# Branch gates of a hybrid decoder layer as seven half-size products for two tiles, in a stage ahead of the mixers

## Chip, cores and metric

The kernel runs on one core of one Trainium2 chip. The time is the device time of one execution in microseconds, as a median of repeated runs. TensorE (PE) multiplies and writes to PSUM; VectorE (DVE), ScalarE (ACT) and GpSimd (POOL) do the elementwise work; SyncE's queue (SP) issues most transfers.

## What is computed

One decoder layer in float32 on 1056 tokens (1024 of a prompt, 32 of a sample group), width 1024. The part that matters, from the reference:

```
h = x + 0.5 * swiglu(rmsnorm(x, g_ffn1), w_ffn1_in, w_ffn1_out)
u = rmsnorm(h, g_mix)
z = split(u @ w_in)                  # attention q, k, v; GLA inputs; memory queries z_mq
o_swa, o_gla, o_mem = mixers(z)      # each (tokens, 512)
mq = z_mq.reshape(B, T, MEM_HEADS, HEAD_DIM)
gates = sigmoid(u @ w_gate).reshape(B, T, N_BRANCH, D_MODEL)     # 3 x 1024 features
br = einsum('btnc,ncd->btnd', stack([o_swa, o_gla, o_mem], axis=2), w_branch)
h = h + sum(gates * br, axis=2) @ w_out
h = h + 0.5 * swiglu(rmsnorm(h, g_ffn2), w_ffn2_in, w_ffn2_out)
y = rmsnorm(h, g_final)
```

## The kernel before

**Layout.** Features lie on the 128 partitions, tokens on the free axis. A slab is one 128 x 1056 buffer; there are 34 (`NSLAB`), given out as they come free. Every float32 product is three matmuls in a reduced format: weights and data are each split into a rounded high part and the rest (`split`, L206 to L209, `weights`, L177 to L192: ACT casts, DVE or POOL subtracts), and `product` (L194 to L204) adds high x high, high x low and low x high. A plain 128-feature tile with depth 1024 is 8 x 3 matmuls for each chunk of tokens: 72 of 352 columns, when the tokens are cut in thirds. Weights come through three pairs of buffers, `raw`, `whi` and `wlo` (`WBUFS`).

**Seven half-size products.** In both feed-forward layers two output tiles a and b are made together from seven products of half depth (`weight_forms`, L395; `pair_products`, L419; the tokens' sums from `Forms.sums`, L365). For each of two pairs of token quarters that is 7 x 12 matmuls of 264 columns, so 168 for two tiles. Their 20 pairs follow on two tiles of each layer that are done the plain way (`plain_products`, L459).

**Stages.** `ffn` (L697) ends with `out_product` (L652), whose last block of depth goes by token thirds, so that `norm_after` (L294) can norm one third while the next is multiplied. Norm steps wait in `k.later` and are taken one at a time with `k.step()`, between products. `Mix.run` (L1620) then makes the projections of u and, between their products, takes a step of five streams with `k.tick()`: GLA, window attention, its sample scores, memory attention, the combination. PE's order is as the program is written; the other engines' orders are made by a planner ahead of time, by readiness and program order. Four memory query projections (`mem_proj`, L1093) are spread over the GLA part. The streams still open when `run` ends are taken on in `gated_branches` (L1650).

**`gated_branches`.** It takes the branches in the order GLA, memory, attention (i = 0, 1, 2), and eight output tiles t in each. For each tile and each third c, `gate` (L1680) makes 24 matmuls on u and a sigmoid on ACT, and `values` (L1690) 12 matmuls on the branch's output; DVE multiplies the two and POOL adds into `merged`. `gate` ticks the streams once, in the first pass (i = 0) twice. At t = 0, and for the last two tiles, three gate products run ahead of the values. At t = 6 of the first pass the streams are flushed and the next branch's output is loaded. The splits `mp` of the merged tiles (L1807) and `w_out` follow.

## Time and profile before

| | |
|---|---|
| median of 3 runs | 3049.06 us |
| lowest and highest | 3039.51 and 3050.46 us |
| profiled execution | 3053.2 us |
| its span, first to last instruction | 3051.4 us |
| matmuls of PE | 21035 |
| PE busy | 2932.9 us |
| granted TensorE clock, mean | 0.975 of 2.4 GHz |

A profiled execution gives each instruction's start and duration. A matmul's duration includes its way through the array, and neighbours overlap; what a matmul costs in a dense stretch is the length of the stretch divided by their count. The clock is granted at 2.4 or 1.2 GHz; a mean between says how the stretch was divided.

### The profile page before, as it was taken

What the parts mean: (1) busy time and instruction counts of PE and PEld (TensorE: products, weight loads), DVE (VectorE), ACT (ScalarE), POOL (GpSimd) and SP (SyncE); (2) the same over time, 40 slices, a digit from 0 to 9 for tenths busy, and PEclk for the clock granted to TensorE, in tenths of its full rate; (3) what the DMA queues carried; (4) which work ended last, traced back from release to release, by engine and by line L of the source; (5) the groups of instructions that cost most, each with busy time, mean ns of one, the idle gap of its engine ahead of it and who ended that gap; (6) DMA issues with size and microseconds to landing.
All of it is one profiled execution on the core that took longest, in us unless ns stands there. A gap on an engine that the chain in (4) does not pass through costs nothing. (4 is left out here: it accounts for less than half of the span.)

```text
span 3051.4 us, 51965 instructions
## 1 busy us (share of the span) xinstructions
PE 2932.9 (96%) x21035; PEld 2867.0 (94%) x21035; DVE 1415.2 (46%) x2581; ACT 1013.6 (33%) x2007; POOL 972.3 (32%) x835
## 2 busy tenths in 40 slices
PE   8999999999999999899998889999999999999999
PEld 7999999899999999888897789999999999999998
DVE  7544444454424445656556551213246544444544
ACT  5433333221345433232332321212234433333212
POOL 4533331110401114637447350112236433332000
PEclk9999999999999999999999889999999999999999
DMA  5222224432211124666566563211252222225322
GB/s 180 80 73 82 78 79 154 151 119 67 92 43 57 58 71 131 174 164 195 150 182 189 166 189 105 81 42 56 75 168 85 78 78 82 73 78 194 96 62 86
DMA packets 455604, 332.88 MB, mean 109 GB/s; under 512 B 34850, under 2 KB 417284, under 8 KB 455364
## 3 DMA queue, kind: packets, MB, share of 16 engines
q1 hardware_dynamic: 445698, 323.44, 34.9%
q10 hardware_dynamic: 9666, 6.11, 0.7%
q8 instruction: 165, 2.70, 0.4%
q14 instruction: 75, 0.61, 0.1%
HBM read 268.88 MB, written 60.60 MB: 108 GB/s over the span
## 5 line engine op out<-in xcount | busy, mean ns | idle before, releaser
L202 PE MATMUL acc<-xh,whi 128*128 128x352 f32 x1776 | 600.0, 338 | 1.4 <-ACT whi L188 1.0
L204 PE MATMUL acc<-xh,wlo 128*128 128x352 f32 x1776 | 587.6, 331 | 8.1 <-DVE wlo L189 8.1
L203 PE MATMUL acc<-xl,whi 128*128 128x352 f32 x1776 | 586.0, 330 | 0.0
L202 PEld LDWEIGHTS acc<-xh,whi 128*128 128x128 f32 x1776 | 345.8, 195 | 13.5 <-issue 9.5
L204 PEld LDWEIGHTS acc<-xh,wlo 128*128 128x128 f32 x1776 | 344.4, 194 | 13.9 <-DVE wlo L189 13.9
L203 PEld LDWEIGHTS acc<-xl,whi 128*128 128x128 f32 x1776 | 345.4, 194 | 0.2
L188 ACT CAST whi<-raw 128x512 fp32r<-128x512 f32 (+2 forms) x200 | 163.3, 816 | 541.1 <-PE acc L203 467.6
L202 PE MATMUL acc<-hh,whi 128*128 128x352 f32 (+2 forms) x968 | 313.8, 324 | 3.0 <-ACT mv L628 1.6
L203 PE MATMUL acc<-hl,whi 128*128 128x352 f32 (+2 forms) x968 | 312.9, 323 | 2.9 <-POOL hl L209 2.1
L204 PE MATMUL acc<-hh,wlo 128*128 128x352 f32 (+2 forms) x968 | 312.9, 323 | 0.9 <-DVE wlo L189 0.9
L189 DVE TENSOR_TENSOR wlo<-raw,whi 128x512 fp32r<-128x512 f32 (+2 forms) x200 | 221.2, 1106 | 176.0 <-ACT whi L188 157.4
L202 PE MATMUL acc<-xs,swf 128*128 128x264 f32 x960 | 276.1, 288 | 8.6 <-ACT u L430 8.6
L203 PE MATMUL acc<-xs,swf 128*128 128x264 f32 x960 | 274.7, 286 | 0.0
L204 PE MATMUL acc<-xs,swf 128*128 128x264 f32 x960 | 274.6, 286 | 0.0
L662 DVE SCALAR_TENSOR_TENSOR h<-acc,h 128x352 f32<-128x352 f32 (+3 forms) x296 | 150.2, 512 | 220.8 <-PE acc L204 219.7
L202 PE MATMUL acc<-xs,whi 128*128 128x264 f32 x768 | 220.9, 288 | 2.5 <-ACT xs L208 1.9
L203 PE MATMUL acc<-xs,whi 128*128 128x264 f32 x768 | 220.8, 288 | 0.8 <-POOL xs L209 0.8
L202 PEld LDWEIGHTS acc<-xs,swf 128*128 128x128 f32 x960 | 182.3, 190 | 9.9 <-ACT u L430 9.9
L202 PEld LDWEIGHTS acc<-hh,whi 128*128 128x128 f32 x968 | 182.8, 189 | 4.3 <-ACT mv L628 1.9
L203 PEld LDWEIGHTS acc<-hl,whi 128*128 128x128 f32 x968 | 182.9, 189 | 3.6 <-POOL hl L209 2.3
L204 PEld LDWEIGHTS acc<-hh,wlo 128*128 128x128 f32 x968 | 182.8, 189 | 1.2 <-DVE wlo L189 1.2
L203 PEld LDWEIGHTS acc<-xs,swf 128*128 128x128 f32 x960 | 182.8, 190 | 0.0
(427 smaller groups left out, 6743.5 us busy)
## 6 DMA issues: line engine op xcount, KB each, us to landing
raw<-in_w_ffn_in SPq DMA_DIRECT2D x88, 512.0 KB, 3.9
raw<-in_w_in SPq DMA_DIRECT2D x52, 512.0 KB, 3.9
kq<-sqt SPq DMA_DIRECT2D x96, 256.0 KB, 5.5
hraw<-hidd SPq DMA_DIRECT2D x44, 528.0 KB, 3.9
raw<-in_w_ffn_out SPq DMA_DIRECT2D x64, 256.0 KB, 2.8
kq<-in_cache_swa SPq DMA_DIRECT2D x64, 256.0 KB, 5.1
vc<-in_cache_swa SPq DMA_DIRECT2D x64, 256.0 KB, 4.6
raw<-in_w_gate SPq DMA_DIRECT2D x24, 512.0 KB, 4.2
```

What stands on the lines that cost most here:

```text
L188: nc.scalar.copy(hi[:, :n], raw[:, :n])
L189: nc.vector.tensor_sub(lo[:, :n], raw[:, :n], hi[:, :n].bitcast(F32))
L202: mm(ps, wh[k], xh[k], start=first and k == 0, stop=False, skip_group_check=more)
L203: mm(ps, wh[k], xl[k], start=False, stop=False, skip_group_check=more)
L204: mm(ps, wl[k], xh[k], start=False, stop=last and k == n - 1, skip_group_check=more)
L662: nc.vector.scalar_tensor_tensor(hv, ps, scale, hv, op0=ALU.mult, op1=ALU.add)
```

## The change

Four things change. (1) Twenty of the 24 gate tiles (`GATE_PAIRS`) are made in pairs by the seven half-size products in a new stage, `early_products`, between the first feed-forward layer and `Mix`; their sigmoids are stored to a scratch tensor `gd` in HBM. (2) The four memory query projections move into the same stage, by token quarters; the other four gate tiles take their places in the GLA part (`gate_proj`, with a tick for each chunk as there). (3) `gated_branches` has no gate products: it loads a slab of gates for each tile, two tiles ahead, ticks in front of each values product, and flushes in the second pass (i = 1) instead of the first. (4) The last block of the first `out_product` goes by token quarters; the norm (`Kept.chunk`) is written over h and split into u's 16 slabs, and `Kept.sums` makes the sums in place, with 16 more slabs for their splits. In the new stage two slabs (`swf`) hold three of the seven weight forms by turns, the last of them made after the fifth product (`late`).

The core of the diff (left out: `norm_after`, `normed` and `store_h` removed, arguments passed on, `sample_queries`, which reads the sample's queries back from scratch):

```diff
+class Kept(Forms):
+    def __init__(self, k):
+        Forms.__init__(self, k)
+        self.parts, self.sum = None, {}
+    def chunk(self, c, h, r, g, in_place):
+        k, nc = self.k, self.k.nc
+        self.parts = self.parts or k.pair("x")
+        for kk in range(KD):
+            nc.vector.scalar_tensor_tensor(h[kk], h[kk], g[:, kk:kk + 1], r, op0=ALU.mult, op1=ALU.mult)
+            k.split(*[v[kk][:, cs(c, 4)] for v in self.parts], h[kk], nc.vector if kk % 2 else nc.gpsimd)
+        self.normed[c] = h
+    def at(self, p, i, j):
+        if j in (0, 1, 6):
+            return [v[i if j == 0 else i + KH][:, cs(2 * p + (j == 6), 4)] for v in self.parts]
+        t, n = self.sum[p, i][j in (2, 5)], (j in (2, 4)) * HC
+        return t[:, n:n + HC], t[:, 2 * HC + n:3 * HC + n]
+    def plain(self, c):
+        return chunk(self.parts, c, 4)
+    def sums(self, p, whole):
+        k, nc = self.k, self.k.nc
+        while self.normed[2 * p] is None or self.normed[2 * p + 1] is None:
+            yield
+        first, x = self.normed[2 * p:2 * p + 2]
+        n = 2 * HC
+        for i in range(KH):
+            x11, x21, x12, x22 = first[i], first[i + KH], x[i], x[i + KH]
+            nc.gpsimd.tensor_sub(x11, x12, x11)
+            nc.vector.tensor_sub(x12, x22, x12)
+            nc.vector.tensor_sub(x22, x22, x11)
+            nc.vector.tensor_sub(x21, x21, x22)
+            s = self.sum[p, i] = [k.slab("xs", F32R), k.slab("xs", F32R)]
+            k.split(s[0][:, :n], s[0][:, n:], whole[i], nc.gpsimd)
+            k.split(s[1][:, :n], s[1][:, n:], whole[i + KH], nc.vector)
+            yield
+        self.normed[2 * p:2 * p + 2] = None, None
+def early_products(k, x, h, wi, cols, outs, pairs, wg, store):
+    nc = k.nc
+    for p in range(2):
+        k.later.append(x.sums(p, [v[:, cs(p, 2)] for v in h]))
+    ws = {}
+    for u in range(2):
+        for c in range(4):
+            while x.normed[c] is None and k.later and (u, c) < (1, 0):
+                k.step()
+            for i in range(2):
+                if c == 0:
+                    ws[u, i] = k.weights(wi[:, :, cols[2 * u + i]:cols[2 * u + i] + 128], KD, 128, slabs=(u, i) == (1, 0))
+                ps = k.acc()[:, :HC]
+                k.product(ps, ws[u, i], x.plain(c))
+                t = k.t264("plain")
+                nc.scalar.copy(t, ps)
+                nc.sync.dma_start(outs[2 * u + i][:, cs(c, 4)], t)
+                k.step()
+    swf = deque(k.slab("swf", F32R) for _ in range(2))
+    for tiles in pairs:
+        w, late = weight_forms(k, *[k.raw_weights(wg[:, :, t * 128:(t + 1) * 128], KD, 128) for t in tiles], swf)
+        def done(what, p, ps, add):
+            if add is None:
+                s = k.t264("gate")
+            else:
+                s = add
+                nc.vector.tensor_add(s, ps, add)
+                ps = s
+            nc.scalar.activation(s, ps, AF.Sigmoid)
+            store(tiles["ab".index(what[0])], cs(2 * p + int(what[1]) - 1, 4), s)
+        pair_products(k, w, x, done, late=late)
...
             t = k.wp.tile([128, 1024], F32R, tag="wlo", bufs=WBUFS[2], name="wlo")
+        elif swf:
+            t = swf[0]
+            swf.rotate(-1)
         else:
             t = k.slab("swf", F32R)
-        k.split(t[:, :n], t[:, n:2 * n], x, nc.vector)
+        make = lambda t=t, x=x: k.split(t[:, :n], t[:, n:2 * n], x, nc.vector)
+        if swf and i == 6:
+            late = make
+        else:
+            make()
         out.append([[t[:, o + j * 128:o + (j + 1) * 128] for j in range(KH)] for o in (0, n)])
-    return out
-def pair_products(k, w, x, done, apart=False):
+    return (out, late) if swf else out
+def pair_products(k, w, x, done, apart=False, late=None):
     for n in range(14):
         j, p = (n % 7, n // 7) if apart else (n // 2, n % 2)
-        if apart and n in (0, 7):
+        if apart and n in (0, 7) or j == 2:
             while x.normed[2 * p] is not None and k.later:
                 k.step()
+        if late and (j, p) == (5, 0):
+            late()
         if j == 0:
             one[p] = k.acc()[:, :HC]
         if j == 3:
...
-    def mem_proj(self, h, mqd):
-        nc, k = self.nc, self.k
-        s = self.proj_copy(COL_MQ + h * E, E, "mq")
-        nc.sync.dma_start(mqd[h * E:(h + 1) * E], s)
...
+    def gate_proj(self, t):
+        k, nc = self.k, self.nc
+        w = k.weights(self.wg[:, :, t * 128:(t + 1) * 128], KD, 128)
+        for c in range(NC):
+            k.tick()
+            ps = k.acc()[:, :C]
+            k.product(ps, w, chunk(self.u, c))
+            s = k.t352("gate")
+            nc.scalar.activation(s, ps, AF.Sigmoid)
+            nc.sync.dma_start(self.gd[t * 128:(t + 1) * 128, cs(c)], s)
...
+        for h in range(H):
+            k.streams[3].append(self.sample_queries(h, mqd))
+        late = [t for t in range(3 * KD) if not any(t in p for p in GATE_PAIRS)]
+        self.gate_proj(late[0])
         z = self.gla_proj(1)
-        self.mem_proj(1, mqd)
+        self.gate_proj(late[1])
         k.flush()
         k.streams[0].append(self.gla(1, *z, on))
-        self.mem_proj(2, mqd)
-        self.mem_proj(3, mqd)
+        self.gate_proj(late[2])
+        self.gate_proj(late[3])
         self.gla_gate(0, on[0])
         self.gla_gate(1, on[1])
...
+GATE_PAIRS = [(t, t + 1) for t in range(0, 3 * KD, 2) if t not in (KD, KD + 2)]
+def gated_branches(k, gd, od, order):
     nc = k.nc
-    wg = k.A["w_gate"][0].rearrange("(k p) f -> p k f", p=128)
     out = [None] * KD
-    late = []
+    gates = deque()
+    tiles = deque(n * D + t * 128 for n in order for t in range(KD))
+    def load_gate():
+        if tiles:
+            g, r = k.slab("gate"), tiles.popleft()
+            nc.sync.dma_start(g, gd[r:r + 128])
+            gates.append(g)
+    load_gate()
+    load_gate()
     def load(n, some):
         raw = [k.slab("oraw") for _ in some]
             if i == 0:
                 out[t] = k.slab("merged")
             if t == KD - 2 and i + 1 < len(order):
-                if i == 0:
+                if i == len(order) - 2:
                     k.flush()
                 raw = load(order[i + 1], range(2))
-            w1 = k.weights(wg[:, :, n * D + t * 128:n * D + (t + 1) * 128], KD, 128)
             w2 = k.weights(wb[:, :, t * 128:(t + 1) * 128], H, 128)
-            def gate(c, w1=w1):
+            load_gate()
+            g = gates.popleft()
+            for c in range(NC):
                 k.tick()
                 if i == 0:
                     k.tick()
-                pg = k.acc()[:, :C]
-                k.product(pg, w1, chunk(u, c))
-                s = k.t352("gate")
-                nc.scalar.activation(s, pg, AF.Sigmoid)
-                return s
-            def values(c, s, w2=w2, t=t):
                 pb = k.acc()[:, :C]
                 k.product(pb, w2, chunk((oh, ol), c))
                 ov = out[t][:, cs(c)]
                 if i == 0:
-                    nc.vector.tensor_mul(ov, pb, s)
+                    nc.vector.tensor_mul(ov, pb, g[:, cs(c)])
                 else:
-                    nc.vector.tensor_mul(s, pb, s)
+                    s = k.t352("value")
+                    nc.vector.tensor_mul(s, pb, g[:, cs(c)])
                     nc.gpsimd.tensor_add(ov, ov, s)
-            if t == 0 or i == len(order) - 1 and t >= KD - 2:
-                ahead = [gate(c) for c in range(NC)]
-                if i == len(order) - 1 and t >= KD - 2:
-                    late.append((values, ahead))
-                    continue
-            else:
-                ahead = None
-            for c in range(NC):
-                values(c, ahead[c] if ahead else gate(c))
-    for values, ahead in late:
-        for c in range(NC):
-            values(c, ahead[c])
     return out
...
-    u, h = [], []
-    def after(c):
-        return norm_after(k, h, g_mix, u)(c)
-    ffn(k, x, A["w_ffn1_in"][0], A["w_ffn1_out"][0], hd[0], h, after, (raw0, raw1),
-        lambda: mem_kv(k, mem_rows(k), g_mem, ktd, vd))
-    store_h(1, h)
-    Mix(k, u[0], od, ktd, vd, g_gla).run()
-    m = gated_branches(k, u[0], od, (1, 2, 0))
+    h = []
+    gd = k.dp.tile([3 * D, T], F32, name="gd")
+    mqd = k.dp.tile([H * E, T], F32, name="mqd")
+    xu = Kept(k)
+    ffn(k, x, A["w_ffn1_in"][0], A["w_ffn1_out"][0], hd[0], h, norm_forms_after(k, h, g_mix, xu, hd[1]), (raw0, raw1),
+        lambda: mem_kv(k, mem_rows(k), g_mem, ktd, vd), spans=QUARTERS)
+    early_products(k, xu, h, A["w_in"][0].rearrange("(k p) f -> p k f", p=128), [COL_MQ + i * E for i in range(H)],
+                   [mqd[i * E:(i + 1) * E] for i in range(H)], GATE_PAIRS,
+                   A["w_gate"][0].rearrange("(k p) f -> p k f", p=128),
+                   lambda t, tokens, s: nc.sync.dma_start(gd[t * 128:(t + 1) * 128, tokens], s))
+    Mix(k, xu.parts, od, ktd, vd, gd, mqd, g_gla).run()
+    m = gated_branches(k, gd, od, (1, 2, 0))
```

## Rows read from the trace of the kernel before

**Rows 1.** The page: busy time of each engine with its share of the span and its instructions; then tenths in 40 slices of the span (each 76.3 us).
```profile
PE 2932.9 (96%) x21035; PEld 2867.0 (94%) x21035; DVE 1415.2 (46%) x2581; ACT 1013.6 (33%) x2007; POOL 972.3 (32%) x835
...
PEclk9999999999999999999999889999999999999999
DMA  5222224432211124666566563211252222225322
```

**Rows 2.** Busy time by stretch: length, then for PE, weight loads, DVE, ACT, POOL the busy us and instructions, the granted clock, the DMA engines' share and GB/s. The 18 pairs of the first feed-forward layer that follow its first pair; the last block of its second product; the start of the mixers.
```profile
107.10:475.90 368.80, 368.80 (x3026) 368.80 (x3025) 153.96 (x270) 142.98 (x307) 127.32 (x107) 1.00 0.26 79
...
752.90:790.30 37.40, 37.40 (x243) 37.38 (x242) 21.95 (x44) 17.13 (x35) 25.41 (x28) 1.00 0.30 111
790.30:850.40 60.10, 57.11 (x349) 55.60 (x348) 18.52 (x27) 17.14 (x34) 13.30 (x12) 0.97 0.21 63
```

**Rows 3.** The same columns for the gated branches: three stretches of the first pass (i = 0; the last stream ends at 1866.6), a dense stretch of the second pass, the end of the third pass, the start of `w_out`.
```profile
1720.60:1764.20 43.60, 29.23 (x166) 27.14 (x165) 20.61 (x51) 21.00 (x47) 11.42 (x8) 0.77 0.53 152
1764.20:1803.50 39.30, 34.42 (x198) 33.26 (x197) 19.27 (x27) 11.21 (x18) 28.36 (x23) 0.91 0.77 239
1803.50:1866.60 63.10, 56.67 (x507) 51.91 (x504) 21.77 (x42) 12.19 (x21) 13.60 (x12) 0.92 0.44 128
...
1948.40:2065.30 116.90, 116.90 (x722) 115.17 (x722) 21.72 (x33) 20.12 (x34) 21.14 (x20) 1.00 0.15 42
...
2170.40:2207.40 37.00, 35.35 (x218) 34.48 (x218) 10.54 (x13) 8.70 (x16) 11.31 (x9) 1.00 0.21 61
2207.40:2264.20 56.80, 53.12 (x433) 52.70 (x433) 25.96 (x32) 20.13 (x34) 23.42 (x19) 1.00 0.60 202
```

**Rows 4.** PE in order of time at the start of the first feed-forward layer, behind a norm (start, us, instruction, in brackets the idle time and what ended it).
```profile
21.41 0.59 PE L202 MATMUL acc<-xs,whi 128*128 128x264 f32 x1 [1.88 <-ACT xs L208]
...
29.07 0.42 PE L204 MATMUL acc<-xs,wlo 128*128 128x264 f32 x1
```

**Rows 5.** PE in order of time at the start of the mixers, by the first weights after the last block.
```profile
796.32 0.43 PE L204 MATMUL acc<-xh,wlo 128*128 128x352 f32 x1 [2.99 <-DVE wlo L189]
```

**Rows 6.** Busy time by stretch, columns as in rows 2, for the first and the second pair of each feed-forward layer.
```profile
79.70:107.10 27.40, 23.81 (x171) 23.09 (x170) 18.40 (x26) 11.61 (x24) 16.88 (x15) 0.88 0.25 73
107.10:127.60 20.50, 20.50 (x171) 20.50 (x170) 10.00 (x17) 8.11 (x18) 9.88 (x8) 1.00 0.22 67
2358.00:2386.70 28.70, 23.21 (x169) 22.37 (x170) 20.33 (x27) 13.05 (x27) 18.55 (x15) 0.94 0.29 88
2386.70:2407.20 20.50, 20.50 (x171) 20.50 (x170) 10.78 (x17) 8.68 (x19) 10.00 (x9) 1.00 0.26 80
```

**Rows 7.** By line and shape in the 18 pairs of rows 2, ACT: count, then busy us and mean ns, then idle time before.
```profile
L208 ACT CAST swf<-ws 128x512 fp32r<-128x512 f32 x36 | 22.3, 620 | 23.8 <-POOL ws L404 13.9 <-PE acc L204 9.9
...
L430 ACT COPY p<-acc 128x264 f32<-128x264 f32 x36 | 13.7, 380 | 26.2 <-PE acc L204 26.2
```

**Rows 8.** The same for DVE.
```profile
L209 DVE TENSOR_TENSOR swf<-ws,swf 128x512 fp32r<-128x512 f32 x36 | 32.9, 914 | 23.3 <-ACT swf L208 23.3
L727 DVE TENSOR_TENSOR u<-acc,u 128x264 f32<-128x264 f32 x72 | 31.0, 432 | 45.4 <-ACT u L430 25.1 <-PE acc L204 18.4
```

**Rows 9.** ACT's instructions by line in the GLA part: count, then busy us and mean ns, then idle time before.
```profile
L217 ACT ACT_TABLE_LOAD x11 | 14.1, 1283 | 0.2
```

**Rows 10.** By line and shape in the dense stretch of the second pass, DVE.
```profile
L1697 DVE TENSOR_TENSOR gate<-acc,gate 128x352 f32<-128x352 f32 x20 | 10.5, 523 | 70.4 <-PE acc L204 70.4
...
L189 DVE TENSOR_TENSOR wlo<-raw,whi 128x512 fp32r<-128x512 f32 x6 | 4.1, 682 | 0.0
```

**Rows 11.** The same for POOL.
```profile
L1698 POOL TENSOR_TENSOR merged<-merged,gate 128x352 f32<-128x352 f32 x20 | 21.1, 1057 | 95.4 <-DVE gate L1697 95.4
```

**Rows 12.** PE's waits while the last streams run, 1720.6 to 1866.6: us in total, times, longest.
```profile
PE aux L1413 <- ACT mp L1141: 4.7, 1, 4.7
PE aux L1494 <- DVE ssc L1482: 4.4, 1, 4.4
PE acc L204 <- DVE wlo L189: 4.4, 2, 3.8
PE aux L1343 <- DVE stat L1348: 3.8, 1, 3.8
PE aux L1554 <- DVE stat L1348: 2.9, 1, 2.9
PE aux L1365 <- ACT v L791: 1.7, 1, 1.7
```

**Rows 13.** PE in order of time at the last head's sample scores: the wait, and the gate product behind it, its first and last matmul.
```profile
1808.77 0.39 PE L1494 MATMUL aux<-ident,ssc 128*32 128x128 f32 x1 [4.40 <-DVE ssc L1482]
...
1809.34 0.66 PE L202 MATMUL acc<-xh,whi 128*128 128x352 f32 x1
...
1815.61 0.32 PE L204 MATMUL acc<-xh,wlo 128*128 128x352 f32 x1
```

**Rows 14.** Waits of the other engines in the first 83 us of it.
```profile
POOL kq L1481 <- DMA kq<-in_cache_swa: 23.7, 6, 8.0
...
POOL og L1614 <- DMA cb<-cd: 12.1, 2, 11.4
```

**Rows 15.** ACT's instructions by line while the last streams run, columns as in rows 9.
```profile
L1687 ACT ACTIVATE gate<-acc 128x352 f32<-128x352 f32 x14 | 6.5, 463 | 34.4 <-PE acc L204 34.3
L1687 ACT ACT_TABLE_LOAD x5 | 6.4, 1283 | 7.8 <-issue 7.4 <-ACT mqo L1173 0.4
```

More of the change, by code (lines that the diff above doesn't have):

```diff
@@ L64 @@
 THIRDS = [cs(c) for c in range(NC)]
+QUARTERS = [cs(c, 4) for c in range(4)]
 SHRINKING = [slice(0, 384), slice(384, 768), slice(768, 928), slice(928, T)]
@@ L263, in spread @@
         return ps[:, :at]
-    def normed(self, h, c, r, g, x):
-        nc = self.nc
-        for k in range(KD):
-            xn = self.t512("xn")[:, :C]
-            nc.vector.scalar_tensor_tensor(xn, h[k][:, cs(c)], g[:, k:k + 1], r, op0=ALU.mult, op1=ALU.mult)
-            self.split(x[0][k][:, cs(c)], x[1][k][:, cs(c)], xn, nc.vector if k % 2 else nc.gpsimd)
     def norm_steps(self, ssq, then):
@@ L291, in pair @@
         return hi, lo
-def norm_after(k, h, g, x):
-    def start(c):
-        ssq = k.new_ssq()
-        def feature(n):
-            k.squares(ssq, h[n][:, cs(c)], n == 0)
-            if n == KD - 1:
-                if not x:
-                    x.append(k.pair("x"))
-                k.later.append(k.norm_steps(ssq, lambda r: k.normed(h, c, r, g, x[0])))
-        return feature
-    return start
 def chunk(x, c, nch=NC):
@@ L398, in weight_forms @@
+def weight_forms(k, a, b, swf=None):
     nc = k.nc
@@ L1089, in transposed, with sample_queries @@
         return [pt[:, j * 128:(j + 1) * 128] for j in range(len(parts))]
[L1093 removed]
+    def sample_queries(self, h, mqd):
         nc, k = self.nc, self.k
[L1095 to L1106 removed]
+        s = k.small("mqs", NS, 128, 2)
+        nc.sync.dma_start(s, mqd[h * E:(h + 1) * E, SEQ:T])
+        yield
+        yield
+        ps = k.aux()[:NS, :E]
+        nc.tensor.transpose(ps, s, k.ident)
+        t = k.small("mqs", E, NS, 2)
+        nc.scalar.copy(t, ps)
+        nc.sync.dma_start(self.mqt[h], t)
+    def gate_proj(self, t):
[8 more added lines that the diff above has]
+            nc.sync.dma_start(self.gd[t * 128:(t + 1) * 128, cs(c)], s)
     def mem_head(self, h, mqd):
@@ L1767, in build @@
     hd = [k.dp.tile([D, T], F32, name=f"hd{i}") for i in range(3)]
-    def store_h(n, h):
-        for i in range(KD):
-            nc.sync.dma_start(hd[n][i * 128:(i + 1) * 128], h[i])
     two = [[k.slab("x") for _ in range(KH)] for _ in range(2)]
```

17 lines of the change are left out of this document (4 added, 13 removed).

## Prediction

> **What bounds the kernel now.** I read the page first: PE is busy for 96% of the span and every other engine for less than half [rows 1]. So a product taken from PE shortens the kernel unless PE then waits instead, and the question for each stage is which of the two it is. The busy share does not answer it, since matmul durations overlap; I therefore took the length of dense stretches by their matmul count. In 18 pairs of the first feed-forward layer 3026 matmuls of 264 columns take 368.80 us, 121.9 ns each; in the second branch pass 722 of 352 columns take 116.90 us, 161.9 ns each [rows 2, 3]. In both the clock is 1.00 and PE busy throughout. The other stretches show where PE is not the bound: the clock row dips in the mixers and at their end [rows 1], and while the last streams run, from 1720.6 to 1866.6, the granted clock is 0.77, 0.91 and 0.92 and the DMA engines are busy for 0.53, 0.77 and 0.44 of the time [rows 3]. The reader is to see there that the first branch pass is not a stretch like the second.
>
> **The change part by part.** The sum is made against the profiled execution, 3053.2 us with 3051.4 us of span; it lies 4.1 us above the median of 3049.06.
>
> Gate products removed: 24 tiles of 72 matmuls, 1728 x 161.9 ns = 279.8 us [rows 3]. Ten pairs added: 10 x 168 x 121.9 ns = 204.8 us [rows 2]. Memory queries by quarters: 4 tiles x 4 quarters x 24 matmuls x 121.9 ns = 46.8 us. The four gate tiles that stay plain stand in the places of the four query tiles, 288 matmuls for 288: nothing. The last block is 216 matmuls by thirds and 288 by quarters, 35.0 and 35.1 us; a fourth norm adds two groups of small matmuls. The block's stretch of 37.4 us [rows 2] holds four such groups beyond its products, 0.6 each, so +1.2. PE's own work: -27.0 us.
>
> One rule of the Trainium skill speaks against this term. The rows give a matmul's cost nearly in proportion to its columns: 121.9 to 161.9 ns is 0.75, and so is 264 to 352. "TensorE: Matmul & The Clock Gate", section "Back-to-back issue gap", gives for pairs of weight load and matmul about 81 ns at 128 columns and 131 ns at 512, which weighs the count more; by a straight line between them (an estimate, about 99 and 110 ns) the change would add 13 us of PE work instead of taking 28 off. The rows at both widths decide against it.
>
> Start of the new stage. The fourth quarter's norm can't lie under the block. Six products, of quarters 0 to 2, stand before its use, but its last small matmul is issued behind them, and then DVE, ACT and POOL make eight features that PE takes at once. The nearest row is the first product of the kernel behind a norm: 1.88 us of wait, then from 21.41 to 29.5 for 24 matmuls that cost 2.9 us when dense [rows 4], though at the lower clock. Bounds 0 and 7; I take +5. The wait of 2.99 us for the first weights after the block [rows 5] goes with the old start, but its cause, two buffers of high and low parts while the block still reads one, meets the second query tile: 0, between -3 and +2.
>
> First pair. The sums need 16 slabs beside u's 16 and h's 8, while there are 34, so the second half's sums wait for h and for the plain weights to come free. The first pair of each feed-forward layer takes 27.4 and 28.7 us, the next 20.5 [rows 6], 6.9 and 8.2 more. Here four products that need no sums stand ahead, against two there. Bounds 0 and 12; I take +6.
>
> The other pairs. The late form is made from the end of the fifth product on: a copy 0.38, a cast 0.62, an add 0.43 and a subtraction 0.91 [rows 7, 8], 2.3 us in a row, under two products of 2.9 us. 0, up to 0.6 a pair. A pair's eight stores move 1.1 MB beside loads of 1.0, in a stretch where the DMA share is 0.26 now [rows 2].
>
> GLA part. The query copy becomes a sigmoid, and tables then change between it and the part's exponentials and logarithms, at 1.28 us [rows 9]. With 12 sigmoids and PE mostly a product ahead I take +2; bounds 0 and 6.
>
> Second and third pass. A tile is 36 matmuls, 5.8 us, on PE; DVE has 3 x 0.52 + 0.68 = 2.3 us [rows 10], POOL 3 x 1.06 = 3.2 us [rows 11]; a gate slab and weights of half the depth are 0.8 MB, or 137 GB/s, where 239 went at a share of 0.77 [rows 3]. PE stays the bound. At each change of branch the splits of its output lose the three gate products that stand ahead of them now, 11.7 us; the loads can be issued a few tiles ahead: +2 for both, bounds 0 and 8. At the end u's 16 slabs are free early, so the merged tiles can be split as they come. Today the last 37.0 us hold 216 matmuls worth 35.0, and the next 56.8 us hold 433 worth 52.8 [rows 3]: 6.0 us lost, of which I take 4 as regained, bounds +2 and -6.
>
> First pass, the term that decides. From 1720.6 to 1866.6 the streams of the last head run: 146 us with 14 gate products, 54.4 us, between their steps. PE's six longest waits there sum to 21.9 us [rows 12]. Taking the gates out leaves 92 us if no wait grows, and 146 if all their time turns into waiting. From the other side, the DMA shares times the lengths give 23 + 30 + 28 = 81 us of full DMA work, which the change does not lessen (a gate slab of 0.54 MB for gate weights of 0.52). Thus 0 to +54, or -11 if waits shrink. What would be late is the chain of sample scores: stored queries, loads of `kq`, POOL's multiply, DVE's sum, PE's transpose at L1494, which comes at 1808.77 after a wait of 4.40 us [rows 13]. Its POOL work waits 23.7 us for cache rows and 12.1 for the combination [rows 14], not for gates. It can move up by the part of attention that gates delay today, some 6 us, and by less crowded queues, to about 75 us after 1720.6, where PE alone would be there at 61: a wait 14 us longer. Five changes of table for sigmoids, 1.28 each, leave ACT [rows 15], which gives back some 4. I take +10, as nearer to the DMA floor than to 146.
>
> Of the clock the rows show that the gate product behind the wait at L1494 takes from 1809.34 to about 1815.8, 6.4 us instead of 3.9, at 1.2 GHz [rows 13]. The same page of the Trainium skill, "Loop structure matters more than you think", leaves it to dense products whether TensorE keeps its clock; by that, thinning this pass lets its remaining 14 values products, 1.9 us each, fall to the lower level, at most 27 us, and the +10 would be +37.
>
> Sum: -27.0 + 5 + 0 + 6 + 0 + 2 + 2 - 4 + 10 = -6. That makes 3047.2 of the profiled execution, and 3043 of the median.
>
> **The rivals.** (A) The last streams hide as well as now. Their waits are ends of chains that gates only delayed, and slabs freed by u let loads run ahead; against it stands DMA at 0.77. First pass -4 instead of +10: 3029. (B) Slower: the first pass is bound by its streams. Place: the sample scores of the last head between 1720.6 and 1866.6, where in-order PE stands at L1494 and at the eight steps of L1546 with 1.9 us of products between steps instead of 5.8. Price: +45 of the possible 54, so 3078. It decides for slower by more than 0.5% once waits there grow by more than 31 us, to over twice today's. For it speak the clock of 0.77 and POOL's waits; against it the DMA floor of 81 and that in the last 63 of the 146 us PE is busy for 57 already [rows 3]. (C) The new stage is not bound by PE. With all 34 slabs taken, every pair costs what a feed-forward layer's first does, 6.9 us more: nine times, 62, so 3105. Against it: one pair's loads and forms leave DVE at 10.0 of 20.5 us [rows 6]. (D) The width saves nothing: at 161.9 ns for 264 columns the stage costs 82.6 us more, 3126. The rows at both widths speak against it; it is the skill's count rule carried to its end.
>
> **How the numbers follow.** Chances: forecast 0.45, A 0.35, B 0.15, C 0.04, D 0.01. A change below 0.5%, some 15 us, can't be told from none. Forecast's own range by the bounds: 3033 to 3060. Faster 0.35 (A), same 0.45, slower 0.20. The range reaches into A's better half at 3014 (more gain at the start and the end) and to B at 3078.
>
> **What would show it.** Right: pairs in the new stage at 20.5 us; 36 matmuls in about 5.8 us in passes two and three; L1494 some 75 us behind the last projection, and about 102 us from there to the last stream. A: under 90 us. B: over 125 us, with waits at L1494 and L1546 at the head of PE's list and the clock below 0.8. C: PE waiting in each pair for ACT or DVE. D: more than 130 ns a matmul in the pairs at full clock. A first pair above 32 us, or waits at the branch changes above 8 us, would put the forecast wrong by a term that I took for small.

## The result and the profile after

The changed kernel is slower: a median of 3078.78 us beside 3049.76 of the kernel before, a ratio on record of 1.011 with a 95% interval of 1.0082 to 1.0139 (the medians alone give 1.0095; four runs of each). The prediction was 3043, most likely no change; slower had 0.20. The profiled execution takes 3076.4 us with 3074.6 of span, 29.2 more than the 3047.2 that the sum gave for it.

The page of the changed kernel, rows as in [rows 1] (40 slices of 76.9 us):

```profile
PE 2919.9 (95%) x21455; PEld 2854.3 (93%) x21455; DVE 1490.5 (48%) x2744; ACT 1077.5 (35%) x2179; POOL 1044.8 (34%) x903
...
PEclk9999999999899998999999999978999999999999
DMA  5222224533223311213555656696352222225312
```

PE is busy 13 us less, yet the span is 23 us longer: the time went into waits. The rows below give busy time by stretch, columns as in [rows 2]. The first is the last block of the feed-forward layer. The next five are the new stage: the first 72 query matmuls; the 72 up to the fourth quarter's norm; the 288 behind it (240 of the queries, and the first pair's 48 that need no sums); the first pair's 96 on sums; the other pairs. Three follow from the last projection on, where the last streams run: up to, in and behind one long wait. Then come all other products of the branches, and the start of `w_out`.

```profile
751.10:798.60 47.50, 42.73 (x326) 42.30 (x325) 34.24 (x77) 21.49 (x51) 32.60 (x42) 0.93 0.33 105
798.60:818.40 19.80, 12.04 (x74) 11.61 (x73) 13.79 (x15) 8.78 (x19) 12.15 (x9) 0.74 0.27 81
818.40:829.60 11.20, 10.18 (x86) 10.09 (x84) 1.14 (x4) 1.97 (x6) 1.27 (x2) 1.00 0.14 47
829.60:871.00 41.40, 38.75 (x289) 38.13 (x290) 18.83 (x31) 14.38 (x32) 15.46 (x15) 0.92 0.19 60
871.00:888.00 17.00, 13.51 (x99) 13.30 (x98) 9.00 (x12) 7.89 (x17) 7.28 (x5) 0.90 0.21 65
888.00:1073.90 185.90, 184.80 (x1515) 184.59 (x1513) 68.03 (x118) 84.15 (x190) 46.33 (x35) 1.00 0.36 110
2005.00:2045.90 40.90, 29.86 (x200) 27.96 (x198) 29.32 (x65) 19.88 (x47) 20.12 (x15) 0.92 0.89 272
2045.90:2066.00 20.10, 0.20 (x4) 0.09 (x3) 10.05 (x12) 0.00 (x0) 19.87 (x17) 0.56 1.07 354
2066.00:2106.20 40.20, 31.32 (x331) 25.27 (x331) 15.58 (x38) 3.22 (x8) 12.29 (x12) 0.75 0.61 190
2106.20:2227.00 120.80, 115.28 (x698) 114.17 (x697) 57.75 (x85) 24.08 (x35) 67.17 (x55) 0.97 0.46 155
2227.00:2283.80 56.80, 53.10 (x421) 52.68 (x420) 25.99 (x32) 20.10 (x34) 23.39 (x19) 0.97 0.58 194
```

The pairs are what the forecast said, 1512 matmuls at 121.9 ns and 1.4 us of waits. The end of the mixers, 101.2 us, is what it said too (102). The loss stands ahead of them: the block takes 47.5 us instead of 37.4 [rows 2], and 72 matmuls that cost 8.8 dense take 19.8 at a granted clock of 0.74. The table has the same by stage, with the forecast's terms put to their places. It gives lengths of PE's stretches in the profiled executions; e9 and e13 are versions of the experiments below. In e13 three values products, 5.8 us, have moved from the row "rest of the branches" into the one above it.

| us | before | forecast | after | e9 | e13 |
|---|---|---|---|---|---|
| last block, feed-forward 1 | 37.4 | 38.7 | 47.5 | 39.0 | 39.0 |
| new stage | - | 262.6 | 278.2 | 268.9 | 266.7 |
| mixers, to the last stream | 1076.2 | 1033.8 | 1029.3 | 1034.1 | 1020.5 |
| rest of the branches | 340.9 | 117.5 | 120.9 | 119.7 | 107.9 |
| `w_out` | 100.5 | 96.5 | 101.9 | 102.2 | 98.0 |
| all else (both feed-forward layers) | 1496.5 | 1496.5 | 1496.8 | 1498.0 | 1496.1 |

The forecast's column sums to 3045.6, its span. Block and new stage miss by 24.4 of 29.0 us, `w_out` by 5.4, the rest of the branches by 3.4; the mixers give 4.5 back. One execution's number for the mixers is good to some 5 us: over the changed kernel and e1, e2, e3, e5, e7 and e9, whose program there is the same, it came out between 1027 and 1036.

What happens at 801: PE of the changed kernel in order of time, and then DVE (start, us, instruction, idle time). Where the text gives one of PE's waits without its row, it counts from the start of the last matmul before it to the start of the next, which is 0.1 to 0.4 us more than the idle time in brackets.

```profile
801.44 0.28 PE L205 MATMUL acc<-xh,wlo 128*128 128x264 f32 x1
803.84 0.39 PE L203 MATMUL acc<-xh,whi 128*128 128x264 f32 x1 [2.12 <-ACT whi L189]
804.07 0.28 PE L204 MATMUL acc<-xl,whi 128*128 128x264 f32 x1
810.00 0.59 PE L205 MATMUL acc<-xh,wlo 128*128 128x264 f32 x1 [5.65 <-DVE wlo L190]
```

```profile
801.29 4.40 DVE L210 TENSOR_TENSOR xs<-h,xs 128x528 fp32r<-128x528 f32 x3
805.61 0.97 DVE L210 TENSOR_TENSOR xl<-h,xh 128x264 fp32r<-128x264 f32 x1
806.50 1.76 DVE L190 TENSOR_TENSOR swl<-raw,swh 128x1024 fp32r<-128x1024 f32 x1
808.18 1.76 DVE L190 TENSOR_TENSOR wlo<-raw,whi 128x1024 fp32r<-128x1024 f32 x1
```

PE is at the second query tile, whose low weights (`wlo`) DVE makes at 808.18. Ahead of them it splits three sums (`xs`), which PE takes 70 us later, and the third tile's low weights (`swl`). The same sums' subtractions (L405 to L408) lie on POOL and DVE in the last block. There PE's longest wait is for the squares of the third quarter (`ssq`), which POOL adds up behind four of these subtractions and the second quarter's low parts (`xl`), PE first and then POOL:

```profile
788.58 0.59 PE L251 MATMUL aux<-ones,ssq 128*128 128x1 f32 x3 [3.98 <-POOL ssq L232]
```

```profile
780.26 1.48 POOL L405 TENSOR_TENSOR h<-h 128x264 f32<-128x264 f32 x2
781.69 0.77 POOL L210 TENSOR_TENSOR xl<-h,xh 128x264 fp32r<-128x264 f32 x1
782.41 1.67 POOL L405 TENSOR_TENSOR h<-h 128x264 f32<-128x264 f32 x2
784.04 2.71 POOL L210 TENSOR_TENSOR xl<-h,xh 128x264 fp32r<-128x264 f32 x3
786.72 1.81 POOL L232 TENSOR_TENSOR ssq<-ssq,sq 128x264 f32<-128x264 f32 x2
```

### The profile page after: what moved, and what is told of

Its sections match the earlier page's. It is cut to its first block, busy times and chain, and to the rows that moved or that the text cites. A ratio compares the mean times of both kernels' runs of the same rounds, so it can differ in the third digit from the quotient of the medians.

```text
span 3074.6 us, 53703 instructions
## 1 busy us (share of the span) xinstructions
PE 2919.9 (95%) x21455; PEld 2854.3 (93%) x21455; DVE 1490.5 (48%) x2744; ACT 1077.5 (35%) x2179; POOL 1044.8 (34%) x903
## 5 line engine op out<-in xcount | busy, mean ns | idle before, releaser
L203 PE MATMUL acc<-xh,whi 128*128 128x352 f32 (+1 forms) x1376 | 463.3, 337 | 3.1 <-ACT whi L189 2.1
L204 PE MATMUL acc<-xl,whi 128*128 128x352 f32 (+1 forms) x1376 | 450.7, 328 | 2.6 <-POOL xl L210 2.3
L205 PE MATMUL acc<-xh,wlo 128*128 128x352 f32 (+1 forms) x1296 | 427.0, 330 | 5.6 <-DVE wlo L190 5.6
L203 PE MATMUL acc<-xs,swf 128*128 128x264 f32 x1120 | 322.2, 288 | 14.0 <-ACT u L497 14.0
L204 PE MATMUL acc<-xs,swf 128*128 128x264 f32 x1120 | 321.2, 287 | 0.0
L205 PE MATMUL acc<-xs,swf 128*128 128x264 f32 x1120 | 321.0, 287 | 0.0
L204 PE MATMUL acc<-hl,whi 128*128 128x352 f32 (+3 forms) x976 | 314.7, 322 | 2.7 <-POOL hl L210 2.1
L203 PE MATMUL acc<-hh,whi 128*128 128x352 f32 (+3 forms) x976 | 315.6, 323 | 0.8 <-ACT mv L697 0.4
L205 PE MATMUL acc<-hh,wlo 128*128 128x352 f32 (+3 forms) x976 | 314.6, 322 | 1.7 <-DVE wlo L190 1.7
L731 DVE SCALAR_TENSOR_TENSOR h<-acc,h 128x352 f32<-128x352 f32 (+4 forms) x304 | 150.8, 502 | 215.8 <-PE acc L205 215.6
L203 PE MATMUL acc<-xs,whi 128*128 128x264 f32 x848 | 244.0, 288 | 1.2 <-ACT xs L209 0.7
L204 PE MATMUL acc<-xs,whi 128*128 128x264 f32 x848 | 243.8, 288 | 0.8 <-POOL xs L210 0.8
L203 PEld LDWEIGHTS acc<-xs,swf 128*128 128x128 f32 x1120 | 213.3, 190 | 15.8 <-ACT u L497 15.8
L204 PEld LDWEIGHTS acc<-xs,swf 128*128 128x128 f32 x1120 | 213.6, 191 | 0.0
L205 PEld LDWEIGHTS acc<-xs,swf 128*128 128x128 f32 x1120 | 213.5, 191 | 0.0
L205 PE MATMUL acc<-xs,whi 128*128 128x264 f32 x720 | 204.8, 284 | 0.5 <-DVE whi L210 0.5
```

What stands on the lines that cost most here:

```text
L203: mm(ps, wh[k], xh[k], start=first and k == 0, stop=False, skip_group_check=more)
L204: mm(ps, wh[k], xl[k], start=False, stop=False, skip_group_check=more)
L205: mm(ps, wl[k], xh[k], start=False, stop=last and k == n - 1, skip_group_check=more)
L731: nc.vector.scalar_tensor_tensor(hv, ps, scale, hv, op0=ALU.mult, op1=ALU.add)
```

## Experiments at the start of the new stage

Theory "start": the 24 us are waits for things made too late behind the sums and the quarters' splits. Rivals: the quarters and the move cost them by themselves, or the engines have too much to do there and a wait only moves. All edits are to the changed kernel; ratios are to the kernel before, on the same chip. The 95% intervals of e1 to e7, e9, e11 and e12 all overlap that of the changed kernel, so a ratio alone tells none of them from it. They are judged by the lengths of the stages that they touch, one profiled execution each; a gain given by the difference of two ratios is an estimate.

**e1**, the first query tile before the second:

```diff
...
+        if u == 0:
+            order = [(c, i) for i in range(2) for c in range(3)] + [(3, 0), (3, 1)]
...
```

> The changed kernel with one edit: of the first two query tiles, the first takes quarters 0 to 2 before the second begins (three products of 2.9 us lie ahead of the second tile's weights, instead of one). In the changed kernel those 72 matmuls took 19.8 us where 8.8 is dense. Theory 'start' (the loss is a wait for the second tile's low weights, 5.9 us, one for its high ones, 2.4, and the clock at 1.2 GHz behind them): the 72 take 9 to 12 us and the kernel gains 8 to 11. Rival 'load' (DVE, ACT and POOL have too much to do between the block and the first pair, and PE would wait a little later for the same work): the wait moves to the fourth quarter's norm or the first pair, and the gain is under 3 us.

Ratio 1.0098 (1.0076 to 1.012). The 72 matmuls took 13.9 us: the wait for the weights is gone, but PE then waits 3.6 for the third quarter's low parts (`xl`), again behind the sums. That is half of the gain that the theory wanted there, and the rest moved as the rival said.

**e2**, five products instead of three ahead of the squares' matmul of quarters 0 to 2:

```diff
-        yield
-        yield
-        yield
+        for _ in range(lead):
+            yield
...
+                                            lead=5 if x.__class__ is Kept and c < 3 else 3))
```

> The changed kernel with one edit: in the last block the squares' small matmul of quarters 0 to 2 is issued behind five products of the next quarter instead of three (a quarter's product is 1.1 us, a third's was 1.46). The block took 47.6 us where the thirds took 37.4. Theory 'start': its waits of 1.07 and 4.27 us and the slow 27 matmuls behind the second go, 6 to 8 us of block and kernel. Rival 'load': the wait stays as long as POOL and DVE are held by the sums of the first half, which here are as early as before, and the gain is 2.2 us or less, what the two extra products cover.

Ratio 1.0091 (1.0068 to 1.0114). The block fell to 41.0: the waits of 1.1 and 4.3 us went, two of 1.2 and 0.7 came, and the slow matmuls behind the long one are gone, so that it is more than the 2.2 us of two products. The wait for the second tile's weights stayed (5.5).

**e3**, the move alone, without sums of tokens (`sums`) and forms of weights (`weight_forms`):

```diff
-        k.later.append(x.sums(p, [v[:, cs(p, 2)] for v in h]))
...
-        pair_products(k, w, x, done, late=late)
+        for c in range(4):
+            ps = k.acc()[:, :HC]
+            k.product(ps, w, x.plain(c))
...
```

> The changed kernel with the twenty gates of the new stage made the plain way, 96 matmuls of 264 columns for each tile, from the same quarters; no sums, no weight forms. It does the move alone. By PE's work, 480 more matmuls of 121.9 ns, 58.5 us for 20 tiles less the 29.3 that the seven products save twice over: 1920 against 1680 matmuls is 240 x 121.9 = +29.3 us. Theory 'start' in the form that the sums' work on DVE and POOL is what makes the block, the query tiles and the first pair wait: these give back 15 to 20, and the kernel is 9 to 15 us slower than the changed one. Rival: the quarters and the moved stage cost that by themselves; only the first pair's 5 us come back, +24.

Ratio 1.0141 (1.0118 to 1.0165), some 8 to 10 us slower than the changed kernel (by the medians and by the spans), for 29 us more of PE work; the theory had 9 to 15, its rival 24. The first two stretches, as above:

```profile
752.10:793.40 41.30, 39.74 (x327) 39.31 (x326) 27.55 (x65) 21.47 (x50) 28.75 (x39) 1.00 0.38 121
793.40:813.30 19.90, 17.06 (x128) 16.85 (x128) 8.03 (x12) 5.22 (x14) 7.70 (x7) 0.91 0.32 95
```

The block needs 6.2 us less, with 4 us less of POOL and 7 of DVE in it, and 72 query matmuls take 13.4. The new stage takes 290.1 us, 9.2 more than its 2304 matmuls at 121.9 ns; in the changed kernel it is 26.6 more than 2064. So sums and forms together cost 6.2 + 17.4 = 23.6 us of block and stage; e3 leaves out both and does not part them. In the block and at the second tile no form is made yet, and the loss there (6.2, and 6.4 of the 72 matmuls) is the sums'. Of the wait for the second tile's low weights 3.1 us stay without them.

**e5**, the sums held behind the fourth quarter:

```diff
-            nc.gpsimd.tensor_sub(x11, x12, x11)
-            nc.vector.tensor_sub(x12, x22, x12)
+            keep = k.tc.keep_in_program_order
+            keep(nc.gpsimd.tensor_sub(x11, x12, x11))
+            keep(nc.vector.tensor_sub(x12, x22, x12))
```

> The changed kernel with the first two subtractions of each sum held behind all that POOL and DVE were given before them, the fourth quarter's norm and splits included; the sums of the first half then start some 50 us later. Theory 'sums' (their DVE and POOL work, taken up as soon as two quarters are normed, is what the last block and the query tiles wait for): the block falls from 47.5 to about 41 us, the first 72 query matmuls from 19.8 to about 13.5, as in the kernel without sums, and the kernel gains 10 to 13. Rival: both halves' sums now meet between the fourth quarter and the first pair, some 16 us of DVE, and the first pair waits for them; the gain is under 4.

Ratio 1.0118 (1.0098 to 1.0138). The block took 41.2 and the 72 matmuls 10.2, as the theory had it, yet the kernel gained nothing: a new wait of 9.3 us stands at the third query tile, and the stage takes 280.6 us, 2.4 more than in the changed kernel.

**e7**, e1, e2 and e5 together:

> The changed kernel with the three edits at the start of the new stage together: the first query tile before the second, five products ahead of the squares' small matmul, the sums behind the fourth quarter. Theory 'start': of the 24 us by which the block, the query tiles and the first pair miss the forecast, 15 to 20 come back, the 72 query matmuls take 9 to 11, and the kernel is about as fast as the one before (within 10). Rival: as the two edits alone gave 4 to 7 each in the stage, the work waits elsewhere and the three together give 10 or less.

Ratio 1.0092 (1.0075 to 1.0109). The block and the first 144 query matmuls with their norm are dense, at full clock:

```profile
748.20:787.20 39.00, 39.00 (x326) 39.00 (x324) 25.68 (x61) 19.89 (x48) 27.95 (x36) 1.00 0.40 130
787.20:806.00 18.80, 18.80 (x159) 18.80 (x158) 7.57 (x15) 6.08 (x17) 7.12 (x9) 1.00 0.25 77
```

PE's waits from 806 to 852 (for what, us in total, times, longest) say where the time went:

```profile
PE acc L203 <- ACT swh L189: 7.7, 1, 7.7
PE acc L205 <- DVE swl L190: 1.6, 1, 1.6
...
```

The third tile's weights now stand behind the sums. The block gave 8.5 us back and the stage took 1.2 more (279.4), so 7.3 in all, as the rival said (10 or less). It is the rival's move of a wait, but the thing that is late can be named, and so be put ahead.

**e9**, e7 with the third tile's weights asked for before the fourth quarter's products:

```diff
...
+            if (u, c, i) == (0, 2, 1):
+                ws[1, 0] = k.weights(wi[:, :, cols[2]:cols[2] + 128], KD, 128, slabs=True)
```

> The three edits at the start of the new stage, and the third query tile's weights asked for before the fourth quarter's products and sums. With the three edits the first two tiles ran dense (72 matmuls in 8.8 us), the block took 39.0, but PE then stood 8.0 and 2.0 us for the third tile's high and low weights, cast and subtracted behind the sums' splits. Theory 'order' (what is late is what stands behind the sums on ACT and DVE, not an engine without time): both waits go, 9 to 12 us of stage and kernel. Rival 'load': the sums end later by as much, and the first pair's waits (6 us there) grow by more than half of what is gained.

Ratio 1.008 (1.0066 to 1.0094). Both waits are gone, 10.5 us of the stage. The stretches of the block, the first 144, the next 288 and the first pair's 96 matmuls:

```profile
753.70:792.70 39.00, 39.00 (x325) 39.00 (x324) 25.74 (x62) 20.35 (x48) 27.99 (x36) 1.00 0.40 130
792.70:813.40 20.70, 19.36 (x159) 18.93 (x157) 9.52 (x19) 6.91 (x20) 7.93 (x8) 1.00 0.33 99
813.40:851.10 37.70, 35.98 (x288) 35.34 (x289) 29.84 (x41) 17.36 (x37) 24.98 (x21) 1.00 0.21 67
851.10:873.30 22.20, 16.04 (x99) 14.70 (x97) 11.76 (x18) 10.29 (x20) 9.51 (x7) 0.85 0.18 53
```

Block and stage together are 17.8 us shorter than in the changed kernel. The whole shows less of it, some 9 us by the ratios and 12.7 by the spans; in these two executions the mixers differ by 4.8 the other way. The first pair's 96 matmuls take 22.1 us, 5 longer than in the changed kernel; behind the sums that are held back its second half's splits come late.

## Experiments at the end of the mixers and after

PE stands 19.9 us for the window sample's scores (L1574), where the kernel before waited 4.4 [rows 13]:

```profile
PE aux L1574 <- DVE ssc L1562: 19.9, 1, 19.9
```

POOL and the DMA engines are both full then (19.87 of 20.1 us, share 1.07). **e4** takes POOL's memory scores to DVE. **e11** leaves out four of the gate slabs' loads (tiles 3 to 6 of the first pass use the second tile's gates, so its result is not the layer's). **e12** does both, and asks for the first two tiles' weights of `w_out` ahead of the splits.

```diff
-                nc.gpsimd.tensor_mul(s[:, m], s[:, 0], kc[:, m, None, :].to_broadcast([128, DT, E]))
+                nc.vector.tensor_mul(s[:, m], s[:, 0], kc[:, m, None, :].to_broadcast([128, DT, E]))
...
+            if KD + 2 <= r // 128 < KD + 6:
+                return
...
+    w_first = [k.weights(wo[:, :, f * 128:(f + 1) * 128], KD, 128) for f in range(2)]
     mp = [[k.slab("mp", F32R) for i in range(KD)] for _ in range(2)]
```

> The changed kernel with the products of the sample's memory scores (POOL, 1.24 us each, 64 in all) on DVE. At the end of the mixers PE stands 20.1 us at the transpose of the window sample's scores, and POOL has no idle time in the last 20 us before it: eight of its own multiplications alternate with nine of the memory scores. Theory 'POOL': the wait falls to 5 to 12 us, and the 101 us from the last projection to the last stream to 88 to 95. Rival 'transfers': cache rows come in that order and rate anyway (the DMA share is highest there); the wait stays within 3 us and the kernel within 3.

> The changed kernel without four of the gate slabs' loads in the first branch pass: tiles 3 to 6 use the second tile's gates again, so those four are left out of the result. Three of the loads are issued while PE waits for the window sample's scores or shortly before. Theory 'transfers': 3 x 0.54 MB at the 353 GB/s of that stretch are 4.6 us, and the wait of 20.1 ends 3 to 6 us earlier. Rival: the wait hangs on the order of issues and on POOL, and stays within 2.

> The changed kernel with edits in two stages that are read apart. (1) At the end of the mixers both loads are taken off together: the memory scores' multiplications on DVE and the four gate slabs not loaded (tiles 3 to 6 use the second tile's gates, so those four are left out of the result). Each alone left the wait for the window sample's scores at 18.7 to 20.1 us, ending 61 to 67 us after the last projection. Theory 'two limits side by side': together they let it end at 52 to 58. Theory 'own pace' (eight steps that each load one ahead): it stays at 61 to 67. (2) The first two tiles' weights of the output projection are asked for ahead of the merged tiles' splits. Theory 'weights': PE's waits of 2.6 and 1.7 us there go, and the projection takes 97 to 99 us instead of 101.9; rival 'splits', as the forecast had it: the second half's splits are late in their turn, and it stays at 101 or more.

Ratios 1.0111 (1.0089 to 1.0133), 1.0147 (1.0132 to 1.0162) and 1.0089 (1.0055 to 1.0124). The wait's stretch in e4, in e11 and in e12:

```profile
2046.80:2067.00 20.20, 0.25 (x4) 0.14 (x3) 18.16 (x24) 0.00 (x0) 9.43 (x8) 0.57 0.91 293
```

```profile
2046.80:2065.50 18.70, 0.25 (x4) 0.14 (x3) 9.67 (x12) 0.00 (x0) 18.38 (x16) 0.58 1.05 345
```

```profile
2041.70:2058.20 16.50, 0.21 (x4) 0.10 (x3) 15.73 (x22) 0.00 (x0) 9.08 (x8) 0.57 1.05 346
```

POOL's work does not by itself set the end: in e4 it is halved, POOL waits for cache rows, and the wait is as long. The transfers stay at 0.91 to 1.05 in all three. But three loads fewer did not bring the end forward either: it comes 61 us after the last projection in the changed kernel, 67, 65 and 64 in these. The engine that takes the work over (DVE, 18.16 of 20.2) is full in its turn. These ends tell little, though. In the experiments at the start, with the same program from the mixers on, the wait ends at 63 and 64 us (e1 and e2, the same order on DVE, ACT and POOL) and at 64 to 75 (e3, e5, e7, e9, where the planner's order differs in places), and is 17.5 to 28.4 us long. Several limits lie close together; which one ends last stays open, and so does why e11, with less to move, is the slowest of the three (waits of 7.4 and 3.9 us follow there). For `w_out` the answer is plain: 97.9 us instead of 101.9, and of its two waits one of 1.4 us remains.

**e6**, another pace of the streams, puts products into the wait:

```diff
-                k.tick()
-                if i == 0:
-                    k.tick()
+                n = t * NC + c
+                for _ in range(1 if i else 0 if 7 <= n < 13 else 3 if 13 <= n < 18 else 2):
+                    k.tick()
```

> The changed kernel with another pace of the streams in the first branch pass: two ticks for each of its first seven values products as now, then none for six products, then three for five, so that the transpose of the window sample's scores, where PE stands 20.1 us, has 13 instead of 7 values products ahead of it. Theory 'transfers' (the wait's end is set by the cache rows, whatever PE does meanwhile): six products of 1.93 us go into the wait, it falls to 8 to 10, and the kernel gains 6 to 11. Rival 'pace': what the streams' ticks issue is itself delayed by the pause; the wait's end moves with it and the gain is under 3.

Ratio 1.0076 (1.0052 to 1.01), some 10 us gained. The wait fell to 13.8 only, its end moving 8 us later, as the rival said. But the later waits for cache rows fell too, and from the first values product to `w_out` PE takes 199.4 us instead of 210.8; the six kernels with the old pace named above took 209.1 to 219.9. The wait's price can be had back in part by filling it, whatever ends it.

## Experiments that put the edits together

**e8** is e7 with e6. **e10** is e9 with e6, and the four slabs of the next branch's output loaded at the seventh tile. **e13** is e10 with `w_first` and the third query tile finished before the fourth begins. **e14** is e13 with plain gates.

```diff
-                raw = load(order[i + 1], range(2))
+                raw = load(order[i + 1], range(H))
...
+        else:
+            order = [(c, i) for i in range(2) for c in range(4)]
```

> The three edits at the start and the pause in the first branch pass together. If both theories hold, 21 to 30 us less than the changed kernel, at or below the kernel before (3036 to 3055 beside 3049). If the gains share a cause (transfers, or the clock) they don't add up and it stays above 3060.

> The former, with the pause in the first branch pass, and with all four slabs of the next branch's output loaded at the seventh tile instead of two there and two at the change of branch (PE waits 2.5 and 1.3 us for their splits there). If theories 'order' and 'transfers' hold and add up: 30 to 38 us less than the changed kernel, 3038 to 3050, within 0.5% of the kernel before. If not, above 3055.

> The kernel with the five edits (three at the start, the third tile's weights early, the pause, the four slabs of branch output), and two more: the third query tile takes its four quarters before the fourth tile begins, so that its two slabs of weights are free 11.7 us earlier, and the output projection's first two tiles of weights are asked for ahead of the merged tiles' splits. In the kernel without these two the second half's sums stop for 13 us for a slab, and the first pair takes 21.6 to 22.2 us where the next takes 11.7 + 8.8 for the same work in turn (its 96 matmuls: 11.7). Theory 'slabs': the 96 matmuls take 13 to 16, and with 4 us at the output projection the kernel gains 9 to 13, 0.3 to 0.5% below the kernel before. Rival 'engines' (POOL's and DVE's own time for sums and weight forms): the first pair stays within 2 us and the gain is 2 to 5.

> The kernel of e13 with the twenty gates made the plain way (no sums, no forms). PE's own work is 240 matmuls of 121.9 ns more, 29.3 us. In the changed kernel the seven products were worth only some 8 to 10 of these. Theory 'order': with the sums out of the way of the query tiles they are worth 20 to 26 here. Rival: the sums' cost is lasting, and it stays at 8 to 14.

e8: 1.0041 (1.0026 to 1.0055), 3055.78 us, just past the upper end of the 3036 to 3055 that it was given if both theories hold. Its interval is clear of e7's and, with 21 us less than the changed kernel by the ratios, the gains of e6 and e7 add up.

e10: 0.9996 (0.9983 to 1.0008), 3041.51 beside 3043.53, inside its 3038 to 3050. The rest of the branches fell from 115.1 in e8 to 108.0 with the earlier loads.

e13: 0.9981 (0.9967 to 0.9994), 3035.98 beside 3041.19, the one version below the kernel before, by 0.2%, less than the 0.5% that the prediction counts as told apart. Its 288 matmuls ahead of the first pair's sums, and the 96 on sums:

```profile
810.80:851.80 41.00, 38.48 (x289) 37.86 (x289) 30.61 (x46) 19.19 (x40) 28.97 (x24) 0.92 0.20 61
851.80:868.40 16.60, 13.74 (x96) 13.22 (x97) 8.30 (x13) 8.38 (x18) 5.97 (x4) 0.90 0.22 60
```

The 96 take 16.7 us instead of 21.6 in e10, short of the 13 to 16 that theory "slabs" wanted. But the 288 ahead of them take 41.0 instead of 39.0, so the stage gained 2.7 us only, and `w_out` 2.6. The whole gained 0.15% against e10, which is the 2 to 5 us of the rival. The stop of 13 us on which that expectation rested is in e7. In e9 and e10 the second half's splits on POOL had come every 4 to 7 us already; in e13 they come every 3.8, each behind a cast of ACT. So the slabs are a part of it, and the rest of the first pair's excess stays open.

e14: 1.0049 (1.0036 to 1.0063), 3057.70. Here the seven products are worth 21.7 us, as theory "order" had it (20 to 26), where in the changed kernel they were worth 8 to 10. In the stage, e14 takes 5.5 us more than its 2304 matmuls, and e13 15.1 more than its 2064: sums and forms still cost 9.6 us there.

## Why the prediction was wrong

**The step that failed** is "Start of the new stage": +5, and 0 for the first weights, with the block at +1.3. The block came out 8.8 us over that, and the stage's first 432 matmuls took 72.4 us for work worth 52.7, a loss of 19.7 instead of 5. The step looked for the trouble at the fourth quarter's norm, and there it was right: the waits at that norm and behind it are 1.3, 1.8, 0.7 and 1.2 us. But it took the sums for a question of slabs alone, due at the first pair. Their subtractions and splits are ready once two quarters are normed, and the planner gives them to POOL, DVE and ACT at once, ahead of the squares, the third quarter's splits and the second tile's weights, which PE takes first. e3 (no sums) and e7 (sums later, tiles in turn) show it: the block takes 41.3 and 39.0, and in e7 the first 144 query matmuls are dense. The bound of 7 for that term came from a stage start that has no such work beside it [rows 4].

**The first weights** were "between -3 and +2". They cost 8.3 us, 2.4 and 5.9, with the clock at 1.2 GHz behind them. e3 and e1 divide them: 3.1 stay without sums, and all of it goes when the first tile takes three quarters first (e1).

**The first pair**: +6 forecast, 5.3 measured. Right in size, by luck: the wait of 3.8 us in it is for PSUM (ACT's copy stands behind a cast of the next pair's weights), not for the slabs that the forecast named.

```profile
PE acc L203 <- ACT u L497: 3.5, 1, 3.5
```

**PE's own work**: right. Pairs at 121.9 ns a matmul, tiles of 36 in 5.8 us. The Trainium skill's count rule ("TensorE: Matmul & The Clock Gate", "Back-to-back issue gap") stays without support in this trace: at 264 columns a matmul costs what it did before.

**First pass**: +10 forecast, 102 us from the last projection to the last stream; 101.2 measured. The scores' transpose came at 61 us instead of 75 and its wait is 15.5 longer than before (forecast 14). Right in size, in part by luck: the forecast had PE there at 61 and the scores at 75, and the runs have 41 and 61. The DMA shares times the lengths give 82 us of full DMA work, beside the 81 that the sum used as its floor; whether the transfers are what binds there is not shown. The fall of the clock that the prediction drew from the Trainium skill (the same page, "Loop structure matters more than you think") is there (0.92, 0.56, 0.75). But the 14 values products took 32.5 us instead of 27.2, so it cost them 5 us at most and not 27.

**End of the branches**: -4 forecast, +1.4 measured. The step took the waits at the start of `w_out` for waits of the splits. The first half's splits did come earlier, one tile at a time; PE still waits 2.6 and 1.7 us for the weights behind the second half's splits, as before. e12 shows it: with the weights asked for first, `w_out` takes 97.9. The branch changes cost 6.5 us of waits, where the forecast had 2; the kernel before had none there, and 2.3 at its last tiles. e10 shows that they were the loads' place.

**The rivals.** The time is within a microsecond of B's, and B is wrong: its place, the last head's scores, lost what the forecast said and not 45 us. A is refuted by the same 101.2 us (it wanted less than 90), C by the pairs, D by their matmuls. None of them gave the start of the stage a mechanism of its own; it was a term among small ones.

**Range and signs.** The range of 3033 to 3060 does not follow from the bounds that it names: with the first pass held at +10, the other bounds add up to 3023 to 3075. And of the signs for being right, the pairs, the 36 matmuls in 5.8 us and the 102 us came true, and only the place of L1494 did not, while the time was wrong. No sign stood at the start of the stage.

## What to carry to other kernels

Work that prepares a later stage is not free because its user is far away: a planner that goes by readiness takes it first, and what PE wants next waits behind it on in-order engines. Cost it where it becomes ready, against what the same engines owe PE there; hold it back, and ask for the next weights ahead of it. Then do it for the whole chain: each of these edits alone gave back about a third of what block and stage had lost, or less, since the next late thing stood right behind. And compare by stage: here the total was that of a rival whose stage did nothing of the kind.

## What the runs showed of the chip

A wait can cost more than its length. The rows show 27 matmuls between two steps of a norm, in the changed kernel's block, ahead of the wait of 4.0 us and behind it (granted clock third from the end):

```profile
774.90:778.20 3.30, 3.30 (x29) 3.30 (x29) 1.48 (x5) 1.56 (x4) 2.76 (x4) 1.00 0.40 130
789.70:795.70 6.00, 6.00 (x28) 6.00 (x29) 4.35 (x12) 0.84 (x2) 3.22 (x4) 0.50 0.19 66
```

PE is busy throughout in both, at 2.4 and at 1.2 GHz: the wait costs 2.7 us more here. In e7, with no wait in the block, the clock is 1.00 throughout. And the DMA engines reach a share of 1.07 at 354 GB/s in the wait at the end of the mixers, where [rows 3] had 0.77 at 239 as the most.
